# Value rows and their taps on GpSimd's DMA queue, and later tap products in the two middle groups

## The chip, the core and the metric

The kernel runs on one core of one Trainium2 chip. The metric is the device time of one execution in microseconds (us), the median of several runs. In the profile, PE is TensorE (its matrix products; PEld are its weight loads), DVE is VectorE, ACT is ScalarE, POOL is GpSimd and SP is SyncE, which here only issues DMA transfers. "SPq" and "POOLq" mark DMA transfers issued by SP and by GpSimd.

## What is computed

One layer of a hybrid decoder trunk over x of shape (1, 256, 2048) in float32. The part that matters here is the front: a normed x goes through one large projection, whose columns are q, k, v, z, two small gates, the input of a pooling mixer and two merge gates. q, k and v pass a causal depthwise convolution of width 4 along the sequence and a silu, and then the gated delta rule.

```python
def causal_dwconv(x, w):                      # width 4 for q, k, v
    width = w.shape[0]
    seq = x.shape[1]
    xp = jnp.pad(x, ((0, 0), (width - 1, 0), (0, 0)))
    y = xp[:, 0:seq] * w[0]
    for j in range(1, width):
        y = y + xp[:, j:j + seq] * w[j]
    return y

h = rmsnorm(x, norm_mix_w[l])
proj = jnp.einsum('bsd,de->bse', h, w_in[l])
q, k, v, z, b_raw, a_raw, p_in, g_a, g_b = jnp.split(proj, splits, axis=-1)
qkv = jax.nn.silu(causal_dwconv(jnp.concatenate([q, k, v], axis=-1), conv_qkv_w[l]))
...
o = gated_delta_rule(q, k, v, g_log, beta).astype(x.dtype)
...
mixed = jax.nn.sigmoid(g_a) * y_a + jax.nn.sigmoid(g_b) * y_b
x = x + jnp.einsum('bsd,de->bse', mixed, w_out[l])
```

There are 16 heads of 128. After this come a second norm, a gated MLP of inner width 5632 (`w_up`, `w_down`) and a final norm. The sequence has 256 positions, kept as two tiles of 128 partitions.

## The kernel before

**Weights and products.** The kernel streams its weights once, as tiles of 128 partitions by 2 x 512 float32 numbers (512 KB, named `raw`, four buffers). SP's queue loads them in the order of use; `load_part` keeps the newest load in `last_load`. ScalarE casts a tile to its high half (`whi`, L255), VectorE subtracts that from the tile and so has the low half (`wlo`, L263). This second step is called a *split* below, and each one is noted in the list `splits`. TensorE makes three passes over each tile in `gemm_a`: high by high (L298), the low half of x by high (L299), high by low (L300), twelve products of 512 columns for one weight tile. Eight such tiles make one projection of 512 columns.

**Groups.** After the first norm the kernel goes over four groups `g` of four heads. In each group the projections for k, q and v come first, then those for the pooling mixer, the z gate and the merge gates. The projections keep TensorE busy. Everything else of a group is "side work", written as Python generators: at each step of the projections one more piece of them is issued. `gdn` is the delta rule of a group: it makes the decay factors (masks by GpSimd, L823), the Gram products of two pairs of heads (L834, L836), their diagonal read-outs on VectorE (L839), a few small operations (L843 to L846, one of them a power on GpSimd, L844), the scaled Gram tiles `ga0` and `ga1` (L853 to L858), a transpose (L883) and a sum (L886), and later a solve.

**The convolution of v.** It needs the rows of v moved by one, two and three positions. Rows lie on partitions, so the kernel moves them through memory: the evicted v projection `e` is written to `vrow` (L1055, SP's queue), and three moved copies `mv` of 512 KB are read back (L740 in `v_moved`, SP's queue). The taps, which are the weights of the convolution, are read as four rows for each group, each spread over all partitions, 256 KB (L724 in `v_taps`, SP's queue); `v_taps` is called just before the v projection. `v_moved` multiplies `e` by the last tap (L735) and notes in `splits_of` how many splits have been issued by then. `v_conv` multiplies each moved copy by its tap (L749) and adds it (L750).

**Order.** A scheduler orders the instructions of each engine when the kernel is built, from dependences and from estimated times. `tc.issue_after(i)` binds it to issue what stands in the block after instruction `i`; it is a rule for the order of issue. The product of copy `n` is bound behind split number `n`, or `n + 3` in group 0, counted from `splits_of`. Each engine and each DMA queue works in order. GpSimd's own DMA queue is used by 24 loads of `w_down` late in the kernel (L208).

Of the kernel before, what the change touches and what calls it, by code (L numbers as in the profile page):

```python
# [14 lines left out]
P = 128  # L15
S = 256
# [9 lines left out]
C_Q, C_K, C_V, C_Z = 0, 2048, 4096, 6144  # L26
# [9 lines left out]
def kernel(  # L36
# [20 lines left out]
    nc = tc.nc  # L57
# [11 lines left out]
    def nm(s):  # L69
        cnt[0] += 1  # L70
        return f"{s}_{cnt[0]}"
# [92 lines left out]
    splits = []  # L164
# [536 lines left out]
    SH = 3  # L701
    vrow = dpool.tile([4, SH + S, 512], F32, tag="vrow", bufs=1, name="vrow")
# [14 lines left out]
    def v_taps(g):  # L717

        taps = []
        for n, tag in enumerate(("sz", "yb")):  # L720
            tp = mp.tile([P, 2, 512], F32, tag=tag, name=nm("taps"))
            for i in range(2):
                with tc.issue_after(last_load[0]):
                    nc.sync.dma_start(tp[:, i, :], conv_qkv_w[0, 2 * n + i, C_V + 512 * g : C_V + 512 * g + 512]  # L724
                                      .partition_broadcast(P))
                taps.append(tp[:, i, :].unsqueeze(1).to_broadcast([P, 2, 512]))
        taps_of[g] = taps
# [3 lines left out]
    splits_of = {}  # L731

    def v_moved(e, g, vt):

        nc.vector.tensor_tensor(vt, e, taps_of[g][3], op=ALU.mult)  # L735
        moved_of[g] = []
        splits_of[g] = len(splits)
        for j in (1, 2, 3):
            m = mp.tile([P, 2, 512], F32, name=nm("mv"), **(dict(tag="cy", bufs=2) if j < 3 else dict(tag="mv")))
            nc.sync.dma_start(m, vrow[g, SH - j : SH - j + S, :].rearrange("(t p) d -> p t d", p=P))  # L740
            moved_of[g].append(m)

    def v_conv(g, vt):

        vt = vt.rearrange("p t h d -> p t (h d)")
        for n, (j, m) in enumerate(zip((2, 1, 0), moved_of[g])):

            with tc.issue_after(splits[splits_of[g] + n + (3 if g == 0 else 0)]):
                nc.vector.tensor_tensor(m, m, taps_of[g][j], op=ALU.mult)  # L749
            nc.vector.tensor_tensor(vt, vt, m, op=ALU.add)  # L750
            yield
        th = mp.tile([P, 2, 512], F32, tag="th", name=nm("th"))
        nc.scalar.activation(th, vt, AF.Tanh)
        yield
        nc.vector.scalar_tensor_tensor(vt, th, 1.0, vt, op0=ALU.add, op1=ALU.mult)
        yield
# [271 lines left out]
    for g in range(4):  # L1028
        kq = mp.tile([P, 4, 2, S], F32, tag="kq", bufs=1, name=nm("kq"))
        for kind, dst in ((1, kq[:, :, 0, :]), (0, kq[:, :, 1, :])):  # L1030
# [13 lines left out]
        res = []  # L1044
        later.append(lambda g=g, kq=kq, vt=vt, res=res, conv=convs[-1]: side_work.__setitem__(
            0, along(gdn(g, kq, vt, v_conv(g, vt), res), conv)))
        v_taps(g)
        if g == 0:
            def after_k(k_conv=k_conv[0]):
# [4 lines left out]
        e = evict(gemm_a(xh, xl, KD), rsh)  # L1054
        nc.sync.dma_start(vrow[g, SH : SH + S, :].rearrange("(t p) d -> p t d", p=P), e)  # L1055
        later.append(lambda e=e, g=g, vt2=vt2: v_moved(e, g, vt2))


# [560 lines left out]
```

## Time and profile before

| | |
|---|---|
| median of 3 runs | 1553.76 us (1552.94 to 1554.03) |
| the profiled execution | 1553.06 us, of which the span of instructions is 1551.3 us |
| TensorE's granted clock, mean | 0.998 |
| data moved by DMA | 310 MB, 200 GB/s on average |
| ScalarE busy | 829.8 us (53%) |
| moved copies, 12 of 512 KB by SP | 4.5 us from issue to landing (median) |
| taps, 16 of 256 KB by SP | 6.5 us from issue to landing (median) |

The span by stages, one row for each stretch. The columns are the stretch in us, its length, the busy time of PE, PEld, DVE, ACT and POOL with the number of their instructions, the granted clock, the mean busy share of the 16 DMA engines, and GB/s:

```profile
0.00:20.00 20.00, 18.94 (x93) 16.36 (x94) 13.32 (x30) 12.43 (x25) 3.10 (x15) 1.00 0.88 305
20.00:60.00 40.00, 40.00 (x190) 32.84 (x190) 30.66 (x65) 24.64 (x41) 4.90 (x8) 1.00 0.79 221
60.00:110.00 50.00, 50.00 (x226) 40.17 (x225) 37.56 (x70) 23.79 (x32) 4.32 (x5) 1.00 0.73 231
110.00:290.00 180.00, 179.50 (x901) 147.47 (x900) 144.08 (x258) 89.79 (x120) 12.66 (x7) 1.00 0.69 199
290.00:470.00 180.00, 178.72 (x895) 146.24 (x894) 143.13 (x252) 88.91 (x118) 8.60 (x7) 1.00 0.67 197
470.00:650.00 180.00, 180.00 (x903) 147.82 (x902) 145.77 (x265) 89.58 (x119) 7.07 (x8) 1.00 0.69 202
```

A line of the timeline begins with the start in us and the duration, then the engine, the line of the kernel, the instruction and its operands (out<-in, partitions x elements); what stands in brackets at its end is the idle time of the engine before it and what ended it. A line of a table of groups has the count (x) and shortest, median and longest duration in ns, then the times of the first and the last. The first products of the four v convolutions (L735) run from 89.0 to 621.0 us.

### The profile page before, as it was taken

How to read it: one execution, taken by the hardware profiler on the slowest of the kernel's cores; microseconds unless marked ns; L12 is line 12 of the kernel's file. 1: busy time of each engine (PE TensorE's matmuls, PEld its weight loads, DVE VectorE, ACT ScalarE, POOL GpSimd, SP SyncE). 2: the span in 40 equal slices, each digit the busy share in tenths (PEclk: the TensorE clock that was granted, in tenths of full speed). 3: DMA queues.
4: the chain of work that ended last, by engine and by line, in shares of the span. 5: the costliest groups of instructions: out<-in, count | busy, mean ns of one | idle time of the engine just before them, and what ended most of it. 6: DMA issues, size and time to landing. Idle time of an engine off the chain costs nothing.

```text
span 1551.3 us, 20145 instructions
## 1 busy us (share of the span) xinstructions
PE 1537.5 (99%) x7350; PEld 1268.2 (82%) x7350; DVE 1195.4 (77%) x1713; ACT 829.8 (53%) x1038; POOL 65.1 (4%) x82
## 2 busy tenths in 40 slices
PE   9999999999999999999999999999999999999998
PEld 8888888788878888888887888888888888788886
DVE  6789858996689858887664877778778776878885
ACT  6455446454545445454454666656656665545552
POOL 1010002000100000000000000000000000000100
PEclk9999999999999999999999999999999999999999
DMA  8777757776577656675676666656666667556652
GB/s 273 212 223 211 199 153 226 213 207 182 166 231 211 197 170 200 215 209 181 215 260 205 189 190 182 186 180 199 203 200 190 188 187 267 189 190 204 221 189 92
DMA packets 167697, 310.46 MB, mean 200 GB/s; under 512 B 19458, under 2 KB 23330, under 8 KB 167470
## 3 DMA queue, kind: packets, MB, share of 16 engines
q1 hardware_dynamic: 159456, 287.37, 61.0%
q0 software_dynamic: 4032, 14.68, 2.9%
q10 hardware_dynamic: 4110, 7.13, 1.4%
q8 instruction: 57, 0.93, 0.2%
q14 instruction: 42, 0.34, 0.1%
HBM read 301.75 MB, written 7.38 MB: 199 GB/s over the span
## 4 chain that ended last, share of the span: by engine, by line
PE 96%; DMA 1%; DVE 1%; issue 1%; ACT 0%; POOL 0%; POOLq 0%; DVEq 0%; ACTq 0%
PE psg L1326 29%; PE psm L298 15%; PE psm L300 15%; PE psm L299 15%; PE psm L1311 7%; PE psg L1311 6%; PE psm L444 1%; PE psm L1383 1%; PE psg L343 1%; PE psm L1326 1%; PE psg L834 1%; DVE wlo L263 0%; DMA raw<-in_w_down_dram 0%; PE psg L836 0%; DMA vrow<-ev 0%
## 5 line engine op out<-in xcount | busy, mean ns | idle before, releaser
L255 ACT CAST whi<-raw 128x1024 fp32r<-128x1024 f32 x460 | 484.1, 1053 | 474.5 <-PE psm L299 277.0
L263 DVE TENSOR_TENSOR wlo<-raw,whi 128x1024 fp32r<-128x1024 f32 x458 | 557.1, 1220 | 169.0 <-ACT whi L255 163.2
L263 DVE TENSOR_TENSOR wlo<-quad,whi 128x1024 fp32r<-128x1024 f32 x112 | 137.1, 1224 | 73.2 <-ACT whi L255 71.9
L255 ACT CAST whi<-quad 128x1024 fp32r<-128x1024 f32 x112 | 118.1, 1055 | 107.5 <-PE psg L1326 55.9
L300 PE MATMUL psm<-wlo,xhl 128*128 128x512 f32 x432 | 169.5, 393 | 1.8 <-DVE wlo L263 1.8
L298 PE MATMUL psm<-whi,xhl 128*128 128x512 f32 x432 | 169.0, 391 | 0.0
L299 PE MATMUL psm<-whi,xhl 128*128 128x512 f32 x432 | 168.6, 390 | 0.0
L1326 PE MATMUL psg<-whi,fhl 128*128 128x512 f32 x504 | 127.9, 391 | 0.0
L1326 PEld LDWEIGHTS psg<-whi,fhl 128*128 128x128 f32 x504 | 93.9, 188 | 18.9
L300 PEld LDWEIGHTS psm<-wlo,xhl 128*128 128x128 f32 x432 | 81.1, 188 | 19.2 <-DVE wlo L263 2.6
L298 PEld LDWEIGHTS psm<-whi,xhl 128*128 128x128 f32 x432 | 81.1, 188 | 16.7
L299 PEld LDWEIGHTS psm<-whi,xhl 128*128 128x128 f32 x432 | 81.1, 188 | 16.7
L1326 PE MATMUL psg<-wlo,fhl 128*128 128x512 f32 x252 | 69.9, 389 | 0.0
L1311 PE MATMUL psm<-wlo,hhi 128*128 128x512 f32 (+1 forms) x150 | 58.1, 387 | 0.5 <-DVE wlo L263 0.5
L1311 PE MATMUL psm<-whi,hhi 128*128 128x512 f32 (+1 forms) x150 | 58.2, 388 | 0.2 <-ACT whi L255 0.2
L1311 PE MATMUL psm<-whi,hlo 128*128 128x512 f32 (+1 forms) x150 | 58.0, 386 | 0.0
L1326 PEld LDWEIGHTS psg<-wlo,fhl 128*128 128x128 f32 x252 | 47.3, 188 | 10.0
L195 DVE TENSOR_TENSOR quad<-quad,quad 128x1024 f32<-128x1024 f32 x40 | 49.0, 1225 | 7.5 <-DMA quad<-in_w_up_dram 6.5
L298 PE MATMUL psm<-whi,mhi 128*128 128x512 f32 x128 | 50.9, 397 | 0.0
L1311 PE MATMUL psg<-whi,hhi 128*128 128x512 f32 (+1 forms) x130 | 50.3, 387 | 0.1
L300 PE MATMUL psm<-wlo,mhi 128*128 128x512 f32 x128 | 50.0, 391 | 0.0
L1311 PE MATMUL psg<-whi,hlo 128*128 128x512 f32 (+1 forms) x130 | 50.0, 386 | 0.0
(428 smaller groups left out, 2939.8 us busy)
## 6 DMA issues: line engine op xcount, KB each, us to landing
raw<-in_w_in_dram SPq DMA_DIRECT2D x224, 512.0 KB, 4.3
raw<-in_w_up_dram SPq DMA_DIRECT2D x136, 512.0 KB, 4.6
raw<-in_w_down_dram SPq DMA_DIRECT2D x64, 512.0 KB, 4.7
quad<-in_w_up_dram SPq DMA_DIRECT2D x40, 512.0 KB, 4.5
raw<-in_w_out_dram SPq DMA_DIRECT2D x32, 512.0 KB, 4.0
quad<-in_w_down_dram POOLq DMA_DIRECT2D x24, 512.0 KB, 5.3
mv<-vrow SPq DMA_DIRECT2D x12, 512.0 KB, 4.5
taps<-in_conv_qkv_w_dram SPq DMA_DIRECT2D x16, 256.0 KB, 6.5
```

The source lines that it names most:

```text
L195: nc.vector.tensor_tensor(out_, plus_, minus_, op=ALU.subtract)
L255: nc.scalar.copy(hi, raw)
L263: last_split[0] = nc.vector.tensor_tensor(lo, raw, hi.bitcast(F32), op=ALU.subtract).ins
L298: mm(ps[:, t, :], lh(k, t), hi[:, kk, :], start=(k == 0), stop=False)
L299: mm(ps[:, t, :], ll(k, t), hi[:, kk, :], start=False, stop=False)
L300: mm(ps[:, t, :], lh(k, t), lo[:, kk, :], start=False, stop=(k == nk - 1))
L343: nc.tensor.transpose(pt[:, ff, t * P : (t + 1) * P], src[:, t, f * P : (f + 1) * P], ident)
L444: mm(ps_k0[:, t, :], part(k, t), w[:, kk, :], start=(k == 0 and w is hi and part is xh), stop=(k == KD - 1 and w is lo))
L834: mm(pg0, kq[:, h, 0, 0:P], kq[:, h, :, :], start=True, stop=True)
L1311: mm(ps[:, cs], lhs(kk), part_[:, kk, cs], start=(first and kk == 0 and n == 0), stop=(last and kk == 1 and n == 2), skip_group_check=shared)
L1326: mm(ps, lhs(kk), w[n][:, kk], start=(first and n == 0 and kk == 0 and lhs is high), stop=False, skip_group_check=True)
L1383: nc.tensor.transpose(out_[f // 2][:, f % 2, t * P : (t + 1) * P], e[:, t, f * P : (f + 1) * P], ident)
```

## The change

It changes three places, all in the convolution of v. The loads of the taps go to GpSimd's queue. The loads of the moved copies go to GpSimd's queue as well. And the tap products of groups 1 and 2 are bound behind the splits two further on: the offset was 3, 0, 0, 0 for the four groups, and becomes 3, 2, 2, 0. The arithmetic is the same.

```diff
@@ v_taps
             for i in range(2):
                 with tc.issue_after(last_load[0]):
-                    nc.sync.dma_start(tp[:, i, :], conv_qkv_w[0, 2 * n + i, C_V + 512 * g : C_V + 512 * g + 512]
+                    nc.gpsimd.dma_start(tp[:, i, :], conv_qkv_w[0, 2 * n + i, C_V + 512 * g : C_V + 512 * g + 512]
                                       .partition_broadcast(P))
@@ v_moved
             m = mp.tile([P, 2, 512], F32, name=nm("mv"), **(dict(tag="cy", bufs=2) if j < 3 else dict(tag="mv")))
-            nc.sync.dma_start(m, vrow[g, SH - j : SH - j + S, :].rearrange("(t p) d -> p t d", p=P))
+            nc.gpsimd.dma_start(m, vrow[g, SH - j : SH - j + S, :].rearrange("(t p) d -> p t d", p=P))
@@ v_conv
-            with tc.issue_after(splits[splits_of[g] + n + (3 if g == 0 else 0)]):
+            with tc.issue_after(splits[splits_of[g] + n + (3, 2, 2, 0)[g]]):
                 nc.vector.tensor_tensor(m, m, taps_of[g][j], op=ALU.mult)
             nc.vector.tensor_tensor(vt, vt, m, op=ALU.add)
```

## The prediction

> **What bounds the kernel now.** I read the head of the page first, then the waits of TensorE's weight loads, then the timeline at the waits found there, then the start of the span by windows.
>
> ```profile
> span 1551.3 us, 20145 instructions
> PE 1537.5 (99%) x7350; PEld 1268.2 (82%) x7350; DVE 1195.4 (77%) x1713; ACT 829.8 (53%) x1038; POOL 65.1 (4%) x82
> PEld psm L300 <- DVE wlo L263: 2.8, 3, 1.7
> ```
>
> TensorE is the bound, and it hardly ever waits. So a change beside the products can gain only what TensorE still loses, and costs whatever makes TensorE wait anew. What it loses to this part of the code is the third line: the pass with the low halves (L300) waits three times, 2.8 us in all, for VectorE's split (L263). The timeline shows two of the three:
>
> ```profile
> 280.69 0.19 PEld L298 LDWEIGHTS psm<-whi,xhl 128*128 128x128 f32 x1
> 282.03 0.19 PEld L300 LDWEIGHTS psm<-wlo,xhl 128*128 128x128 f32 x1 [0.92 <-DVE wlo L263]
> 458.87 0.19 PEld L298 LDWEIGHTS psm<-whi,xhl 128*128 128x128 f32 x1
> 460.99 0.19 PEld L300 LDWEIGHTS psm<-wlo,xhl 128*128 128x128 f32 x1 [1.70 <-DVE wlo L263]
> 275.93 1.23 DVE L749 TENSOR_TENSOR mv<-mv,taps 128x1024 f32<-128x1024 f32 x1 [2.65 <-DMA mv<-vrow]
> 452.47 1.23 DVE L749 TENSOR_TENSOR mv<-mv,taps 128x1024 f32<-128x1024 f32 x1 [4.56 <-DMA mv<-vrow]
> 271.44 1.39 SPq L740 DMA_DIRECT2D mv<-vrow  x3
> 448.78 1.39 SPq L740 DMA_DIRECT2D mv<-vrow  x3
> ```
>
> They lie in groups 1 and 2. VectorE stands at the first tap product (L749) until the moved copy lands, 2.65 and 4.56 us, and the splits queued behind it come late. Together 0.92 + 1.70 = 2.6 us: all that the change can win there, 0.17% of 1553.06, the profiled execution's own time (its span and 1.8 us around it). This execution lies 0.70 us below the median of the runs, 1553.76; I add the sum to the median at the end.
>
> **Two more splits ahead of the products (groups 1 and 2).** In the instruction lists of the two builds this also moves the Gram products of the second pair of heads (L834, L836) from behind three or four weight tiles to behind the tile that used to wait, and on VectorE their read-outs (L839) and the transpose L883 to ahead of two later splits. No work is added; VectorE has the same work after the moved copy lands, in another order, so I count it out. The rows:
>
> ```profile
> quad<-in_w_up_dram SPq DMA_DIRECT2D x40, 512.0 KB, 4.5
> quad<-in_w_down_dram POOLq DMA_DIRECT2D x24, 512.0 KB, 5.3
> DMA to landing us min/median/max: 4.3/5.3/8.3
> L208 POOL DMA_DIRECT2D quad<-in_w_down_dram x24: 722/722/909, 1266.0 to 1474.4; - x24
> 277.07 0.28 DVE L839 CUSTOM_DVE_ANT_0 jk<-psg,ident 128x128 f32<-128x128 f32 x1
> 283.03 0.17 DVE L845 RECIPROCAL sj<-ssk 128x4 f32<-128x4 f32 x1
> 286.57 0.47 DVE L853 SCALAR_TENSOR_TENSOR ga<-psg,sj,dec 128x256 f32<-128x256 f32 x1
> 289.05 3.47 DVE L263 TENSOR_TENSOR wlo<-raw,whi 128x1024 fp32r<-128x1024 f32 x3
> 289.67 0.19 PEld L298 LDWEIGHTS psm<-whi,xhl 128*128 128x128 f32 x1
> 292.72 0.19 PEld L300 LDWEIGHTS psm<-wlo,xhl 128*128 128x128 f32 x1
> ```
>
> The issuing queue comes first. The same 512 KB tile takes 4.5 us from SP and 5.3 from GpSimd (24 of them: 4.3 to 8.3), so the first moved copy is there at 271.44 + 5.3 = 276.7 and 448.78 + 5.3 = 454.1.
>
> Group 1, VectorE from there to the end of the split that becomes critical (of the fourth tile from the one that waits now): ten full-width operations at 1.13 (three in 3.47, the last 1.2 long) make 11.3; the six ga operations 2.5 (286.57 to 289.05); three read-outs and three small ones at 0.28 and 0.17, 1.3; the split itself 1.2. That is 16.3, so 293.0. TensorE wants it at 280.69, plus three tiles (289.67 − 280.69 less the 0.9 of the wait, 8.1), plus two products 0.45, plus the four Gram products, which now stand ahead of it (292.72 − 289.67 − 0.45 = 2.6): 291.8. It waits 1.2 us, where it waited 0.92; the wait at the old place goes, since the Gram products fill it.
>
> Group 2 the same way: twelve full-width operations 13.6, ga 2.5, seven read-outs and three small ones 2.5, the split 1.2: 19.8, so 473.9. TensorE: 458.87 + four tiles at 2.7 + 0.45 + 2.6 = 472.7. It waits 1.2 us where it waited 1.70.
>
> So 2.4 us stay of 2.6: −0.2. Each microsecond of landing time moves both sums by one: at 4.3 us the term is −2.2, at 8.3 it is +5.8. I take 5.3, the median of the nearest transfers.
>
> **Groups 0 and 3.** Their split counts stay; only the queue changes.
>
> ```profile
> 106.62 1.22 DVE L263 TENSOR_TENSOR wlo<-raw,whi 128x1024 fp32r<-128x1024 f32 x1
> 109.53 0.19 PEld L300 LDWEIGHTS psm<-wlo,xhl 128*128 128x128 f32 x1
> 637.94 0.19 PEld L300 LDWEIGHTS psm<-wlo,xhl 128*128 128x128 f32 x1
> 621.01 0.37 SPq L1055 DMA_DIRECT2D vrow<-ev  x1
> 624.65 1.39 SPq L740 DMA_DIRECT2D mv<-vrow  x3
> ```
>
> Group 0 has 109.53 − 107.84 = 1.7 us in hand and loses 0.8. In group 3 the list puts half of the eviction and one weight load ahead of the row write, which I price at 1 us: 624.65 + 1 + 5.3 = 631. Then come three full-width operations and four small ones, 4.2, and the split, 1.2: 636.4, before 637.94. Both cost nothing, and 0.9 and 1.5 us more of landing time would be covered too.
>
> **On the queues.** SP loses 28 issues; no weight load is late today, so that is worth nothing, and I count no gain. GpSimd gets them. Behind each wait for the row write stand only the key norms (L844), used much later at L915; the masks of dec (L823) come ahead of the copies. 0.72 us each of GpSimd costs nothing there.
>
> **The taps of group 0 at the start.** This is where I expect the time to go. On SP these four loads stood behind a weight load, in queue order, at 49.73. Moved to GpSimd, nothing keeps them there: in the list of the changed build the first stands between the fill of half (L695) and ident (L351), three behind idb (L568), all four without a wait.
>
> ```profile
> 49.73 1.88 SPq L724 DMA_DIRECT2D taps<-in_conv_qkv_w_dram  x4
> 1.17 0.09 POOL L695 MEMSET half<- 128x2 f32 x1
> 1.99 1.90 POOL L568 TENSOR_SCALAR_AFFINE_SELECT idb<-ones 32x256 f32<-32x256 f32 x4
> 5.00:20.00 15.00, 15.00 (x78) 12.68 (x77) 10.57 (x18) 10.96 (x23) 0.00 (x0) 1.00 1.00 363
> 53.00:58.00 5.00, 5.00 (x24) 4.14 (x23) 4.71 (x11) 2.63 (x4) 1.58 (x2) 1.00 1.04 171
> taps<-in_conv_qkv_w_dram SPq DMA_DIRECT2D x16, 256.0 KB, 6.5
> ACT whi L230 <- DMA raw<-in_w_in_dram: 0.9, 1, 0.9
> L179 SPq DMA_DIRECT2D raw<-in_w_in_dram x1: 368/368/368, 11.7 to 11.7; - x1
> DMA to landing us min/median/max: 7.0/7.0/7.0
> 19.67 1.07 ACT L255 CAST whi<-raw 128x1024 fp32r<-128x1024 f32 x1
> L735 DVE TENSOR_TENSOR vt<-ev,taps x4: 1211/1216/1227, 89.0 to 621.0; 128x1024 f32<-128x1024 f32 x4
> ```
>
> So they are issued at about 1.3 us and, idb ending at 3.9 and one issue of 0.9 ahead of it, from 4.8 to 7. The DMA engines are full from 5 to 20 us (share 1.00, 363 GB/s) with x and the first weights, and the first casts wait for them. The later loads have about a microsecond in hand: the one issued at 11.7 lands at 18.7 and is cast at 19.67. What do four tap loads take from full engines? By bytes 4 × 0.262 MB / 363 GB/s = 2.9 us. But just after they were issued on SP the engines stayed full (1.04) at 171 GB/s instead of 363: 5 us × 192 GB/s = 0.96 MB, another 2.6 us; all 128 partitions read the same row. Together 5.5 us of all engines, less the 1.0 in hand: TensorE starts its products 4.5 us late in sum, and being the bound never wins that back. The bounds are 0 (served only where engines are free) and 5.5. At 49.73 nothing waited for the taps, so leaving there wins nothing. The 0.9 us by which ident comes later has the runup products over it.
>
> Sum: +4.5 − 0.2 = +4.3: 1557.4 for an execution like the profiled one, 1558.1 for the median.
>
> **Two rules of the Trainium skill that speak against the change.** The row: the 24 GpSimd issues took 722 to 909 ns, with VectorE 77% busy. "SBUF — State Buffer", in the part on the "DVE blocks DMA" trap, says that a DMA from GpSimd's queue can wait for its descriptors while VectorE runs in a mode that takes both ports. By the rule the first copy could come one full-width operation later, 1.2 us, in groups 1 and 2, and the sum would be +6.7; by the row it is +4.3, and the issues show no such stretch. The second: the clock column shows 1.00 at the start. "TensorE: Matmul & The Clock Gate", in the part on the HAM clock gate, says that after an idle window of about 3.4 us the array runs at half clock until it has been busy as long again; by that a start wait in one piece costs an estimated 1.7 us more. No row here shows it.
>
> **The rivals.**
> - *Start hidden.* The engines serve the taps beside the weights without delaying any by more than the 1.0 us in hand. Then the term of groups 1 and 2 is left: −0.2, down to −2.2 with landings of 4.3. For it: nobody needs these taps before 89.0 us (L735). Against it: full engines. It decides at 1.0 us of engine time. I put it at 1553.0, 0.24.
> - *Start half as dear.* Without the same-row slowness 2.9 − 1.0 = 1.9, so +1.7: 1555.5, 0.16. For it: taps mixed with other packets may not crowd one row.
> - *Faster.* Start hidden and both waits gone, with a better order around them as well: below 1550.7. The row of waits gives at most 2.6, which alone isn't enough. 0.05.
> - *Clock or late copies on top.* The start as forecast, and TensorE's clock falls in the wait (as the waits are spread over several loads, mostly not), or a copy lands 2 us later than 5.3 in each middle group, +4: 1559.8 to 1562. 0.12.
> - *The change doesn't do what it says.* The taps of group 0 stay late because GpSimd's first DMAs start only after a long set-up. It would look like the first rival and is counted there.
>
> **How the numbers follow.** The forecast, 1558.1, gets 0.43. This kernel's three runs lie within 0.07%, so 0.2%, 3.1 us, is about what can be told from no change: slower begins at 1556.9. Slower: the forecast's share above that (0.43, less 0.02 for a start under 3.3) and the 0.12, with a little of the half-dear case: 0.56. Faster 0.05; same 0.39. The range runs from 1552.0, which takes in the hidden start with most of its landings, to 1561.0.
>
> **What would show it.** In the changed profile: four tap issues on GpSimd before 8 us; engines full to about 25 us; TensorE's first gaps between 6 and 20 us, 4.5 in sum; L300's waits near 292 and 473 (plus the shift) of about 1.2 each and none at the old places. I am wrong in the main term if the loads of x and the first weights land as before although the taps were issued, and in the second if L300 waits nowhere in groups 1 and 2 or the copies land well away from 5.3.

## The result, and the profile after

The changed kernel takes 1570.22 us (median of 4, 1567.32 to 1571.56), the kernel before beside it 1553.89 us (4 runs, 1552.94 to 1556.22): the ratio is 1.0097, 95% interval 1.0081 to 1.0113. It is slower by 16.3 us. The forecast was 1558.1 with a range of 1552.0 to 1561.0: the sign was right, the size was not. The profiled execution took 1570.52 us, its span is 1568.7 us, 17.4 more than before.

From the page of the changed kernel, its head and two of its DMA rows (count, size, median us from issue to landing):

```profile
span 1568.7 us, 20185 instructions
PE 1544.2 (98%) x7350; PEld 1267.1 (81%) x7350; DVE 1192.9 (76%) x1713; ACT 830.8 (53%) x1038; POOL 88.5 (6%) x110
...
mv<-vrow POOLq DMA_DIRECT2D x12, 512.0 KB, 8.5
taps<-in_conv_qkv_w_dram POOLq DMA_DIRECT2D x16, 256.0 KB, 6.6
```

The 8.5 us from GpSimd's queue are the median of all twelve copies. The 4.5 us of SP's are the median of only four, two first and two second copies, since the profile tells no landing of the others. Like for like, the first copies of the four groups took 7.5, 7.2, 5.5 and 6.9 us from GpSimd's queue. From SP's they took 4.1, 4.5, 3.7 and 4.3 us; the last two are read from the start of VectorE's first tap product, which waited for the copy. From the waits (total us, times, longest), those of TensorE for the splits in the changed kernel, then those of VectorE for the copies in the kernel before and in the changed one:

```profile
PEld psm L300 <- DVE wlo L263: 14.7, 21, 3.3
```
```profile
DVE mv L749 <- DMA mv<-vrow: 10.8, 4, 4.6
```
```profile
DVE mv L749 <- DMA mv<-vrow: 21.5, 4, 5.9
```

TensorE's row was 2.8 us in 3 waits and is 14.7 in 21. Where they stand, from the timeline of the changed kernel, at the products and at VectorE's wait for the first copy of groups 1, 2 and 3:

```profile
110.59 0.19 PEld L300 LDWEIGHTS psm<-wlo,xhl 128*128 128x128 f32 x1 [1.47 <-DVE wlo L263]
285.41 1.22 DVE L749 TENSOR_TENSOR mv<-mv,taps 128x1024 f32<-128x1024 f32 x1 [5.87 <-DMA mv<-vrow]
289.63 0.30 PEld L834 LDWEIGHTS psg<-kq 128*128 128x128 f32 x2 [2.26 <-issue]
301.83 0.19 PEld L300 LDWEIGHTS psm<-wlo,xhl 128*128 128x128 f32 x1 [1.23 <-DVE wlo L263]
463.70 1.23 DVE L749 TENSOR_TENSOR mv<-mv,taps 128x1024 f32<-128x1024 f32 x1 [4.13 <-DMA mv<-vrow]
646.34 1.23 DVE L749 TENSOR_TENSOR mv<-mv,taps 128x1024 f32<-128x1024 f32 x1 [5.84 <-DMA mv<-vrow]
651.59 0.29 PEld L300 LDWEIGHTS psm<-wlo,xhl 128*128 128x128 f32 x1 [3.26 <-DVE wlo L263]
```

Comparing when TensorE reaches the same weight load in the two traces splits the 17.4 us by place: 2.4 by 30 us of the span (the start), 3.9 more in group 0, 2.7 in group 1, 1.4 in group 2, 5.1 in group 3, and 1.9 in all that follows. Each trace is one execution, and a group can differ by up to 2 us between executions without any change in it (run 9 shows such a case).

The start, from the windows of the changed kernel in the columns of the first table, the stretch that was shown of before:

```profile
5.00:20.00 15.00, 13.18 (x67) 9.97 (x66) 8.61 (x15) 8.63 (x18) 1.61 (x3) 1.00 1.02 366
```
```profile
1.51 0.71 POOL L724 DMA_DIRECT2D taps<-in_conv_qkv_w_dram  x1 [0.25 <-issue]
...
4.87 1.75 POOL L724 DMA_DIRECT2D taps<-in_conv_qkv_w_dram  x3
```

The second fence is GpSimd's timeline: the taps left at 1.51 and 4.87 to 6.6 us, as the prediction had it from the instruction list. The engines were full, at 366 GB/s, and TensorE lost 2.4 us there.

Group 3 holds something more. The windows of the changed kernel around its longest wait (the third number from the end is the granted clock):

```profile
648.00:651.50 3.50, 0.75 (x4) 0.29 (x2) 3.47 (x7) 1.05 (x1) 2.08 (x1) 0.97 0.10 34
651.50:654.50 3.00, 2.91 (x7) 2.33 (x8) 3.00 (x7) 0.00 (x0) 0.00 (x0) 0.50 0.59 158
```

Behind the wait of 3.26 us TensorE's clock was granted at half, in the trace from 651.3 to 654.7 us: weight loads stood 0.43 us apart instead of 0.23. That is 1.4 of the 5.1 us.

### The profile page after: what moved, and what is told of

Same layout as the page of the kernel before. It is cut to its first block, busy times and chain, and to the rows that moved or that the text cites. A ratio compares the mean times of both kernels' runs of the same rounds, so it can differ in the third digit from the quotient of the medians.

```text
span 1568.7 us, 20185 instructions
## 1 busy us (share of the span) xinstructions
PE 1544.2 (98%) x7350; PEld 1267.1 (81%) x7350; DVE 1192.9 (76%) x1713; ACT 830.8 (53%) x1038; POOL 88.5 (6%) x110
## 4 chain that ended last, share of the span: by engine, by line
PE 87%; DMA 5%; DVE 3%; issue 2%; SPq 1%; ACT 1%; POOLq 0%; POOL 0%; DVEq 0%; ACTq 0%
PE psg L1326 29%; PE psm L300 13%; PE psm L298 12%; PE psm L299 12%; PE psm L1311 7%; PE psg L1311 6%; DVE wlo L263 1%; DMA lb<-cdd 1%; DMA mv<-vrow 1%; DMA vrow<-ev 1%; PE psm L444 1%; PE psm L1383 1%; PE psm L1326 1%; PE psg L343 1%; DMA x<-in_x_dram 1%
## 5 line engine op out<-in xcount | busy, mean ns | idle before, releaser
L208 POOL DMA_DIRECT2D quad<-in_w_down_dram x24 | 17.4, 725 | 591.4 <-DVE wlo L263 454.6
```

The costliest lines, as they stand in the source:

```text
L208: nc.gpsimd.dma_start(r, down[2 * half + int(what[1]) - 1][2 * chunk + int(what[0]) - 1])
```

## The experiments

**Theories.** A: the copies land late because they now share the DMA engines with weight loads of SP's queue, which no longer waits for the row write; the splits queued behind the tap products are late in turn. B: the offsets, and the order that they bring, cost it. D: GpSimd's queue is slow by itself. S: the start costs what the taps add there.

**1. The taps alone.**

```diff
-                    nc.sync.dma_start(tp[:, i, :], ...
+                    nc.gpsimd.dma_start(tp[:, i, :], ...
```

> Only the 16 tap loads go to GpSimd's queue; copies and offsets as before. If the start is all that the taps cost, TensorE is late by the 2.35 us that the changed kernel shows there (L604 at 44.5 instead of 42.2 us) and by nothing after that: +2.4 us, about 1556.3. Rival: the taps of groups 1 to 3 also disturb the weights or GpSimd's masks, then it is +4 or more, and the extra shows as new waits of TensorE near 250, 430 or 612 us.

Measured: 1558.97 us (6 runs), ratio 1.0031 (1.0019 to 1.0043), +5.3, which is more than was expected. The rival's new waits near 250, 430 and 612 us are not there. The trace has 2.8 us at the start, 0.5 in the groups, 1.6 at 828 us and 1.0 at the end. The 1.6 us are the clock again, after a wait (L1212) that every version has. The windows of the 4 us behind that wait, in the kernel before and then with the taps moved:

```profile
828.00:832.00 4.00, 4.00 (x21) 3.35 (x20) 1.63 (x3) 2.01 (x3) 0.00 (x0) 1.00 0.83 258
```
```profile
831.00:835.00 4.00, 4.00 (x14) 3.24 (x15) 0.97 (x2) 1.41 (x3) 0.00 (x0) 0.63 0.73 230
```

The wait has the same 2.71 us in both. In 8 of the 14 profiled executions of this study the clock fell behind it, in 6 it did not; so these 1.6 us belong to no change. The start is what the taps are seen to cost; whether the 0.5 and the 1.0 us are theirs too is not told apart.

**2. The copies alone.**

```diff
-            nc.sync.dma_start(m, vrow[g, SH - j : ...
+            nc.gpsimd.dma_start(m, vrow[g, SH - j : ...
```

> Only the 12 moved copies go to GpSimd's queue; taps on SP, offsets 3, 0, 0, 0. Theory A (the copies land late because weight loads of the other queue share the DMA engines with them): first copies land 5.5 to 7.5 us after their issue instead of 4.1 to 5.2, as in the changed kernel, and the groups lose at least what they lose there, 3.9, 2.7, 1.2 and 5.3 us, since the products come no later: +10 to +18 us, 1564 to 1572. Theory B (the offsets and the order that they bring do it): the copies cost at most 0.8 us a group, +3 us or less.

Measured: 1573.67 us (4 runs), ratio 1.0139 (1.0124 to 1.0154), +20.0. First copies landed 6.9 to 7.3 us after issue. By group the loss is 2.6, 3.4, 4.9 and 4.9 us. B falls: the copies alone cost more than the whole change. The landings are what A expected, the total is a little above its range; A and D are not told apart here. Part of the loss is the clock: behind TensorE's waits of 2.71, 3.89 and 3.48 us in groups 1, 2 and 3 it was granted at half for 3.4 us each time, which is an estimated 1.7 us of loss each (half of 3.4).

**3. The offsets alone.**

```diff
-            with tc.issue_after(splits[splits_of[g] + n + (3 if g == 0 else 0)]):
+            with tc.issue_after(splits[splits_of[g] + n + (3, 2, 2, 0)[g]]):
```

> Only the offsets change, 3, 0, 0, 0 to 3, 2, 2, 0; all loads on SP. Theory A: the landings stay at 4.1 to 5.2 us, the waits of 0.9 and 1.7 us in groups 1 and 2 go or move; but in its order SP has one weight load more ahead of the row write of group 3, which makes that write 2 to 3 us later: between -2.6 and +3 us, 1551.3 to 1557. Theory B: it carries most of the loss, +8 us or more.

Measured: 1554.11 us (11 runs), ratio 1.0003 (0.9995 to 1.0012). No difference, and B falls again. In its trace the waits at about 281 and 460 us are gone; against the kernel before TensorE wins 0.8 us between 105 and 615 us, and loses 0.8 in group 3, where the row write is issued behind one weight load more. Differences of this size in one execution prove nothing alone.

**4. The change without the early taps.**

```diff
-                    nc.gpsimd.dma_start(tp[:, i, :], ...
+                    (nc.sync if g == 0 else nc.gpsimd).dma_start(tp[:, i, :], ...
```

> The changed kernel with the taps of group 0 alone back on SP's queue, behind a weight load. The start then goes as before and everything later as in the changed kernel: 2.35 us less than the changed kernel, about 1567.9, +14 us on the kernel before. If the start had cost more than the shift at 42 us shows, or if the later groups depend on it, the difference is not 2.4.

Measured: 1567.36 us (5 runs), ratio 1.0087 (1.0073 to 1.0100), +13.7. The start is as before (0.8 us earlier, in fact), and the groups still lose: 4.4, -0.3, 2.2 and 5.1 us. The first copies landed after 8.1, 4.6, 6.4 and 6.4 us: the one group that loses nothing is the one whose copy was in time. With the run of the copies alone this says what the offsets did inside the change: they took back some 6 of the 20 us that the copies cost (the taps of groups 1 to 3, which differ too, cost at most 0.5 us in the groups in run 1). Part of it is the clock, which fell in three groups of the trace of run 2 and in one here.

**5. Later products.**

```diff
-            with tc.issue_after(splits[splits_of[g] + n + (3, 2, 2, 0)[g]]):
+            with tc.issue_after(splits[splits_of[g] + n + (6, 6, 6, 6)[g]]):
```

> The changed kernel with the tap products of all groups bound behind splits 6 further on instead of 3, 2, 2, 0. Theory A (the copies land late, and the splits queued behind the products pay): the first copy lands some 13 us after the row write, which is five weight tiles of 2.7 us, so the splits go ahead and the waits for wlo near 109, 154, 300, 482 and 648 us go; what stays is the start, 2.4 us, and the tail: 1556 to 1559. Rival C (VectorE has too much to do in that stretch, wherever the products stand): the waits only move, and it stays above 1565.

Measured: 1568.39 us (4 runs), ratio 1.0097 (1.0080 to 1.0114), the same as the changed kernel. The expectation of the time failed, that of the waits did not: by 700 us TensorE was 2.0 us behind the kernel before, which is less than the start's 2.5. Then it lost 10.3 us at once. From TensorE's waits and its timeline in this run:

```profile
PEld psg L944 <- DVE T L920: 7.4, 2, 6.6
...
PEld psm L300 <- DVE wlo L263: 2.6, 4, 0.8
```
```profile
725.41 0.18 PEld L944 LDWEIGHTS psg<-T,ga 32*32 32x32 f32 x2 [6.64 <-DVE T L920]
```

The solve of the last group (L920 turns its result) stands behind the convolution, and behind the last group no other group's work hides it. Lateness that groups 0 to 2 hid was paid in group 3. The two waits at L944 are 7.4 of the 10.3 us; most of the rest is the clock, which was granted at half from 722.9 to 733.2 us.

**6. SP's weights behind the row write.** Copies on GpSimd as in run 2, and:

```diff
+        hold[0] = nc.sync.dma_start(mark[g : g + 1], vrow[g, SH + S - 1 : SH + S, 0:128]).ins
...
-        last_load[0] = nc.sync.dma_start(loads[n][:, k], srcs[n][:, k]).ins
+        with tc.issue_after(hold[0]) if hold[0] is not None else ExitStack():
+            last_load[0] = nc.sync.dma_start(loads[n][:, k], srcs[n][:, k]).ins
```

> Copies on GpSimd's queue, taps on SP, offsets 3, 0, 0, 0 as in the run of the copies alone; and SP reads 512 bytes of the written rows ahead of its next weight load, so that its weights wait for the row write as they did when SP issued the copies. Theory A (sharing): the row write and the copies meet no older weight loads, the row write lands sooner than 6 us after its issue, and the first copies land nearer 4.5 than 7 us: of the 20 us that the copies alone cost, at least half comes back (1558 to 1564). Theory D (GpSimd's own queue is slow, whatever else runs): the copies land as late as before, 7 us, and at most the row write's share comes back: 1568 or more.

Measured: 1574.47 us (4 runs), ratio 1.0133 (1.0118 to 1.0149). Nothing came back, and both theories missed something. The row write now took 3.3 us to the issue of the first copy, against 6.3 to 6.8 in the changed kernel; the first copies still took 6.3 to 7.2 us, since the held weight loads left in the same moment. And the weights were late: TensorE waited 11.7 us for casts (L257 here), which it did not before. This run alone doesn't separate A from D.

**7. SP's weights behind the copies.** As run 6, but with this line behind the copies in place of run 6's first:

```diff
+        hold[0] = nc.sync.dma_start(mark[g : g + 1], m[127:128, 1, 384:512]).ins
```

> As the run before, but SP reads 512 bytes of the last copy, so no weight load is issued until all three copies have landed. The total is not the point (weights will be late). Theory A: with the engines to themselves the first copies land in 4 to 4.5 us and all three, 1.57 MB, in about 5 us after the last issue. Theory D: the first copy still takes 5.5 us or more.

Measured: 1585.49 us in a single execution (late weights, as meant). The first copies landed after 4.1, 4.1, 4.0 and 4.0 us. Here are the queues' rows (packets, MB, share of the engines) from 276 to 284 us of this run, then from 278 to 290 us of the changed kernel, both from the issue of group 1's copies on; q0 is GpSimd's queue, q1 is SP's:

```profile
q0 software_dynamic: 432, 1.57, 57.7%
q1 hardware_dynamic: 2, 0.00, 0.0%
...
mv<-vrow POOLq DMA_DIRECT2D x3, 512.0 KB, 4.9
```
```profile
q0 software_dynamic: 432, 1.57, 38.0%
q1 hardware_dynamic: 560, 1.07, 26.2%
...
mv<-vrow POOLq DMA_DIRECT2D x3, 512.0 KB, 8.6
```

The same three copies, from the same queue: 4.9 us (median of the three) with the engines to themselves, 8.6 with 1.07 MB of weights between their packets. D falls, A holds. How the engines divide themselves is left open; it was not evenly: in the first 4 us from that issue in the changed kernel 0.40 MB of copies passed and 0.69 MB of weights.

**8. The copies on ScalarE's queue.** `nc.scalar.dma_start(m, vrow...)` in place of run 2's edit.

> The copies on ScalarE's queue, a hardware queue like SP's, taps on SP, offsets 3, 0, 0, 0; ScalarE's casts stand behind the wait for the row write, so the total is not the point. Theory A: where SP's weight loads are under way beside them, the copies land in 5.5 us or more, as from GpSimd. Theory D: they land in 4.1 to 5.2 us, as from SP.

Measured: 1560.92 us in a single execution. The first copies landed after 5.7, 4.9, 5.5 and 6.1 us in the four groups (the third read from VectorE's start, which waited for it). So a third queue, a hardware one, lands late beside SP's weights too, three times as A expected and once between the theories. It is less late than GpSimd's, but fewer weights passed beside it: in the six us from the issue of group 1's copies 0.56 MB, in run 2 0.92. So the run does not say whether the kind of queue has a share in it.

**9. Offsets that leave group 3's order alone.** The offsets 3, 2, 1, 0 in the kernel before.

> The kernel before with offsets 3, 2, 1, 0 and all loads on SP. With 3, 2, 2, 0 the two old waits went (1.5 us won by 500 us of the span) but the row write of group 3 was issued behind one weight load more; here it keeps its place. If that place is what gave the win back in group 3: 1.5 to 2.6 us below the kernel before at 660 us of the span, and 1551 to 1552.5 in all. If the win was only a scatter of one execution: within 1 us of the kernel before.

Measured: 1553.96 us (11 runs), ratio 0.9998 (0.9990 to 1.0007). A miss, and within the 1 us that was expected of a scatter: the row write keeps its place in group 3 and nothing is lost there, but group 2 still waits 0.7 and 1.0 us for splits, at new places, and group 0 loses 2.0. Its instructions stand in the same order as in the kernel before; in this execution its first copy landed after 5.3 us instead of 4.1.

**10. The taps behind the first norm.**

```diff
-                with tc.issue_after(last_load[0]):
-                    nc.sync.dma_start(tp[:, i, :], ...
+                with tc.issue_after(last_pow[0]):
+                    nc.gpsimd.dma_start(tp[:, i, :], ...
```

> Only the taps on GpSimd, as in the run of the taps alone, but bound behind GpSimd's own power for the first norm (L537), which waits for all of x; so they can't leave in the first microseconds. If the start is what they cost, the 2.8 us at 30 us of the span are gone, and it is within 1.5 us of the kernel before (1552.5 to 1555). Rival: a later cost of these loads, then it stays at 1557 or more.

Measured: 1554.38 us (12 runs), ratio 1.0005 (0.9997 to 1.0014). GpSimd's timeline in this run:

```profile
32.56 0.70 POOL L537 TENSOR_TENSOR rs<-ms,epsx 128x2 f32<-128x2 f32 x1 [28.67 <-DVE ms L535]
33.23 2.35 POOL L724 DMA_DIRECT2D taps<-in_conv_qkv_w_dram  x4
```

The loss is gone. The order "behind a weight load" had no hold on another queue; an order behind an instruction of the same engine has.

**11. The change, repaired.** Taps as in run 10, offsets 6, 6, 6, 0, copies of group 3 on SP.

> The changed kernel, repaired where the runs put its cost: taps on GpSimd bound behind the power for the first norm; copies of groups 0 to 2 on GpSimd with products 6 splits further on, copies of group 3 on SP with offset 0. If the start, the late landings and the end of group 3 are all of the cost: 1551 to 1556. If group 3 stays late for another reason, or the clock falls in a wait, 1558 or more.

Measured: 1558.43 us (8 runs), ratio 1.0027 (1.0014 to 1.0039): most of the cost is repaired, not all. In its trace TensorE is 1.0 us behind at 615 us and 4.0 behind at 735: the third copy of group 3 is issued at 633.6, 8 us after the second, behind more weight loads.

**12. The same offsets with all loads on SP.**

> The kernel before with offsets 6, 6, 6, 0 and all loads on SP. The waits of groups 1 and 2 (2.6 us) should go, as with the later products on GpSimd's queue, without the start and without late copies: 1551 to 1553. But in its order one copy of each group is issued behind two weight loads more; in group 3, where the products follow at once, that copy is late and TensorE waits for a split there: then 1554 to 1558.

Measured: 1557.61 us (12 runs), ratio 1.0020 (1.0010 to 1.0030). The second half of the expectation: 1.2 us ahead at 615 us, of which 0.9 are from the start, and 5.0 behind at 735. The third copy of group 3 was issued at 632.7. In the last stretch the clock fell once (721.4 us). No version of the study beats the kernel before.

## Why the prediction was wrong

**The step that failed is the landing time of the copies, and with it "Groups 0 and 3 cost nothing".** I priced a copy from GpSimd by the 24 loads late in the kernel, 5.3 us. First copies took 7.5, 7.2, 5.5 and 6.9. The queue alone wasn't slower (run 7: 4.0). I also counted it as only 0.8 us more than SP's (5.3 less 4.5), though the 4.5 mixes first and second copies. What I overlooked is what SP did while it waited. Before, its copies stood ahead of the next weight loads in one queue, and what was issued behind them came behind them:

```profile
q1 hardware_dynamic: 608, 1.16, 75.3%
issues: line engine op xcount, KB each, median us to landing
mv<-vrow SPq DMA_DIRECT2D x3, 512.0 KB, 4.5
raw<-in_w_in_dram SPq DMA_DIRECT2D x2, 512.0 KB, 8.8
```

That is the kernel before, 271.4 to 276 us: 4.5 for the first copy, 8.8 for a weight load issued behind the copies (one landing of each is told). TensorE did not wait for those weights. On two queues it is the other way round, and the copies are what is waited for. I had written that SP's 28 issues were "worth nothing"; they were the copies' right of way. The Trainium skill has the rule in "DMA: Bandwidth & Descriptors", section "Queues, rings and completion order": each DMA engine goes round between the queues that have work, a packet of each at a time. Run 7 agrees as far as it goes (8.6 us shared, 4.9 alone); the turns themselves no run here shows. It would have named the right rival.

**Groups 1 and 2.** My count gave 1.2 us of waiting at each new place: for 5.3 us of landing. With 7.2 group 1 waited 2.26 at the Gram products, which came late too, and 1.23 at the split: TensorE lost 2.7 on the kernel before, not 0.3. Group 2 landed at 5.5, about as I forecast, and still lost 1.4, so there the count itself failed: at the forecast place it waited 0.98 us (483.5 us of the span), near my 1.2, but 0.71 stayed at the old place (469.0), where I had put nothing, and 0.99 came at 501.6. My upper end, +5.8 at 8.3 us, would have held both groups.

**Group 0.** In hand were 1.7 us. The first copy landed 7.5 us after issue, where SP's took 4.1, and 2.4 us of TensorE's shift apart it was issued 1.0 us later: 4.4 late, less 1.7, is 2.7. TensorE lost 2.3 in its first two waits there (1.47 and 1.06 us), and the other 1.6 at later splits, up to 155 us.

**Group 3.** I put the row write 1 us later and the landing at 5.3, and so the split at 636.4, 1.5 us ahead of need. The write took 6.7 us to the issue of the copies, not 3.6: it was issued 0.85 us behind a weight load (631.95, 632.80), before 2.6 us behind one (618.42, 621.01). Then 6.9 us of landing. The 3.26 us wait that came of it cost 1.4 more by the clock.

**The start.** The forecast of 4.5 was mis-sized: 2.4 here, 2.8 in run 1. The cause and the issue times were right; the same-row term (2.6 us) was not there. With the taps among the loads the engines moved 366 GB/s, not less than the 363 before. By bytes alone, 2.9 us less some of the cover, it comes out: this was the rival "half as dear", +1.9.

**The clock.** I cited the Trainium skill's "TensorE: Matmul & The Clock Gate", on the HAM clock gate, with 1.7 us for a wait in one piece, and said that no row shows it. The change made such a wait, in group 3: half clock for 3.4 us, 1.4 us lost. The Trainium skill's page speaks of a free-running window of about 3.4 us. The traces agree with that length: the falls of run 2, at 286.79, 471.11 and 652.02 us, are 54 and 53 times 3.41 us apart. That the window need be idle they don't bear out. Here are such windows, laid out from each execution's own falls, around the wait of 2.71 us: two of the kernel before, where the clock held, then two of run 1, where it fell:

```profile
822.93:826.34 3.41, 2.32 (x13) 1.71 (x11) 2.77 (x5) 2.10 (x4) 0.70 (x1) 1.00 0.87 237
826.34:829.76 3.42, 2.04 (x11) 1.79 (x12) 1.26 (x3) 1.27 (x3) 0.00 (x0) 1.00 0.86 265
```
```profile
828.63:832.05 3.42, 1.11 (x7) 1.04 (x8) 1.71 (x3) 1.24 (x3) 0.00 (x0) 1.00 0.79 223
832.05:835.46 3.41, 3.41 (x9) 2.63 (x9) 0.97 (x2) 1.45 (x3) 0.00 (x0) 0.50 0.69 230
```

In the kernel before the wait lies across two windows, and TensorE is busy for 2.32 and 2.04 us of them. In run 1 it lies in one, which leaves 1.11 us of work, and the next window has half the clock. So where a wait falls decides, and one shorter than a window is enough.

**The other rule.** The Trainium skill's "SBUF — State Buffer" has VectorE holding up GpSimd's descriptors (the "DVE blocks DMA" trap). Nothing here needs it: the issues of the copies took 707 to 760 ns, and those of run 7 landed in 4.0 us.

**The rivals.** "Clock or late copies on top" was the right kind, at 0.12, and too small: it had copies late by 2 us on 5.3 in two groups, not in four, and gave no cause. Summed by place, forecast against measured: start +4.5, +2.4; groups 0 to 3 together -0.2, +13.1; the rest 0, +1.9, in which the profile shows a late weight at 1486 us (1.4 us) that is no part of the change as far as the runs tell.

## What to carry to other kernels

A transfer on the queue of a busy load stream also has its place in that stream: what is issued behind it comes behind it. Moving an urgent transfer to a free queue frees the issuer, but gives the engines over to both; so ask what the old queue will send while the urgent bytes fly. And an order of issue binds only within one queue: a load that is moved to another needs a new reason not to leave at the start.

## What was not expected of the hardware

GpSimd's queue delivered 512 KB in 4.0 to 4.1 us with the engines free, as fast as SP's first copies (3.7 to 4.5 in the kernel before). A 512 KB write took 2.8 us alone (run 6) and 6.1 behind weight loads. And a wait of 2.71 us of TensorE can halve its clock for 3.4 us: in 8 of 14 executions it did, which alone spreads two runs of one kernel by 1.6 us.
